# A second ring for the values' pages, moved head stores and loads, and shifted operands in a hybrid attention block

## The chip, the cores and the metric

The kernel runs on one core of one Trainium2 chip. The metric is the device time of one execution in microseconds (us). A kernel's time is the median of its runs; beside it stands one execution taken with the hardware profiler, which has a time of its own.

## What is computed

One layer of a streaming encoder over 512 tokens with 2048 channels, all in float32:

```python
h = rms_norm(x, norm_mix_w)
q_a, k_a, v_a, q_g, k_g, v_g, r_g, gate_lr = split(h @ w_in)
y_a = chunked_band_attention(q_a, k_a, v_a, bias)       # 16 heads of 64, softmax
o_g = gated_linear_attention(q_g, k_g, v_g, log_a)      # 4 heads, state passed over chunks of 64
y_g = rms_norm(o_g) * silu(r_g)
x = x + concat(y_a, y_g) @ w_out
u = causal_depthwise_conv(rms_norm(x) @ w_ffn_up)
x = x + (gelu(u_gate) * u_val) @ w_ffn_down
x = x + sigmoid(rms_norm(x) @ w_ple_gate) * (p @ w_ple_proj)
return rms_norm(x)
```

## The kernel before

**Products.** TensorE (PE) is given each large product as Winograd's seven products of 2x2 blocks (names P1, P2, P6, P5, P7, P3, P4). A *unit* is two blocks of 128 output channels by 512 tokens; its seven products are seven *steps*. Every float32 operand is split in two float32r halves, hi and lo, and a product is made of three passes (hi by hi, hi by lo, lo by hi): 24 matmuls of 256 columns. ScalarE (ACT) writes a weight block's hi half into a `wsplit` page, VectorE (DVE) the lo half, two steps ahead of use (`prep_high`, `prep_low`). Partial results wait in PSUM banks `accA`, `accB`, `accC`; `collect` adds them up in the unit's output page `u`.

**Stages.** First `vproj` makes the linear heads' values and a small gate projection, `plr`. The linear stage then runs units 16, then 20 and 21 as a pair, 17, then 22 and 23 as a pair, 18, 8, 19. Units 16 to 19 are keys and queries of the four linear heads, each followed over ten steps by its head's recurrence (`gla_head`), which stores its result `og` in the scratch `ond`. Units 20 to 23 are the attention's values (`value_product`): here the weights stream through the array and the activations are the part held in it, the other way round than everywhere else. Their results go to two pages `vo`, one for each half of the tokens (h = 0 and 1), and then to the scratch `vad`. Units 8 to 11 are output gates: `after_gates` loads a head's result (`on`) from `ond` and multiplies by it. The front stage runs the attention's eight units 0 to 7 (`attend`) and the gates 9 to 11. Four `PP` steps (`embedding`) follow, then the `wo` stage, the feed-forward stages and the last gate stage. i0 is the first step of unit 11; the `PP` steps are i0+7 to i0+10.

**Pages and rings.** Pages of 4 KB a partition are handed out by rings in turn. In the linear and front stages ring `u` has two pages (u0, u1), for the units' outputs and both `vo` pages; ring `x` has one (r6), for `on` and for `tp`, sums of operands on their way to scratch; ring `c` has one (c0). From the end of the attention on, ring `c` has c1, c2, c0, and hands out two `on` pages, `pT` (the embedding's input), and the `pp_o` pages of the embedding's results. A page is written anew only when its last reader, a store's DMA too, is done.

**Order.** PE, ACT and DVE run in the order in which the steps and an `agenda` of (step, place in the step) write the work down. SyncE (SP) and GpSimd (POOL) only start DMAs; their order is set by the framework's scheduler, and each of their queues is worked through in order, an entry that waits holding those behind it.

**Addresses.** A `wsplit` page has 48 columns more than its contents; `SHIFT` says from which column on it is used, 3 by default, 35 for the values, 48 for the embedding. The built program puts these pages at a multiple of 256 bytes plus 192, and the activations' pages, K and Q of the attention at a multiple of 256 plus 128.

Of the kernel before, what the change touches and what calls it, by code (L numbers as in the profile page):

```python
# [15 lines left out]
T = 512  # L16
# [15 lines left out]
PLAIN = ("P1", "P2", "P6", "P5", "P7", "P3", "P4")  # L32
HALVES = ("P1", "P2", "P6", "P7", "P4", "P5", "P3")
RINGS = {"wr": ("r0", "r1", "r2"), "w": ("w0", "w1", "w2")}
SHIFT = {"v": 35, "pp": 48}
SPLIT = (P, 2096)
FRONT_RINGS = {"u": ("u0", "u1"), "c": ("c0",), "x": ("r6",)}
BACK_RINGS = {"u": ("u2", "u3", "u0", "u1"), "c": ("c1", "c2", "c0"), "x": ("x0", "x1")}
# [5 lines left out]
def encoder_block(ctx: ExitStack, tc: tile.TileContext, A, out):  # L44
# [52 lines left out]
    def page(ring, name, dt=F32, shape=(P, 1024)):  # L97
        tags = rings[ring]
        i = counts.get(ring, 0)
        counts[ring] = i + 1  # L100
        tag = tags[i % len(tags)]
        return page_pool(tag).tile(list(shape), dt, tag=tag, name=name)
# [8 lines left out]
    def psum_mm(name):  # L111
        return pm.tile([P, T], F32, tag="mm", name=name)

    def psum_aux(name):
        return aux[0](name)
# [403 lines left out]
    def value_collect(unit, prod):  # L519
        if unit.half == 0:  # L520
            return
        b = PRODUCTS[prod][2]
        tag, t = unit.banks[b]
        unit.lead.left[b] -= 1
        if unit.lead.left[b] == 0:
            banks.append(tag)
        quarter, sign = QUARTERS[prod]
        s, h = int(quarter[1]) - 1, int(quarter[2]) - 1
        if h not in unit.pages:
            unit.pages[h] = page("u", "vo").rearrange("p (j f) -> p j f", j=2)  # L530
        for j in range(2):
            dst, src = unit.pages[h][:, j, s * 256:s * 256 + 256], t[:, j * 256:j * 256 + 256]
            r = (rtok if sign > 0 else gla["minus"])[:, 2 * h + j:2 * h + j + 1]
            if quarter not in unit.have:
                act.activation(dst, src, AF.Copy, scale=r)
            else:
                vec.scalar_tensor_tensor(dst, src, r, dst, ALU.mult, ALU.add)
        unit.have.add(quarter)
# [199 lines left out]
    def attend(unit):  # L738
# [3 lines left out]
        def tile_(name, cols, dt=F32, tag=None, bufs=1):  # L742
            return att[0].tile([P, cols], dt, tag=tag or name, name=name, bufs=bufs)
# [12 lines left out]
        def high():  # L756
            for n in ("Q", "Kh", "Kl"):
                for s in range(2):
                    M[n, s] = tile_(f"{n}{s}", T, F32R)
            for s in range(2):  # L760
                a = slice(s * 64, s * 64 + 64)
                act.activation(M["Q", s][a], o[a, 0, :], AF.Copy, scale=0.125)
                for r in (a, slice(64 - s * 64, 128 - s * 64)):
                    act.activation(M["Kh", s][r], o[a, 1, :], AF.Copy)
# [73 lines left out]

    tails = [None, None]

    def after_gates(unit):
        g, M = unit.u - 8, {}

        def load():
            M["on"] = page("x" if g < 2 else "c", "on").rearrange("p (s t) -> p s t", s=2)
            nc.sync.dma_start(M["on"], ond[g])

        def times():
            vec.tensor_tensor(unit.o, unit.o, M["on"], ALU.mult)

        def pair():
            ops = store_pair(mixd if g < 2 else None, 4 + g, unit.o[:, 0, :], unit.o[:, 1, :])
            if g >= 2:
                tails[g - 2] = ops

        return [(0, 0, load), (0, 1, lambda: vec.tensor_tensor(unit.o, unit.o, rb2, ALU.mult)),
                (0, 2, lambda: act.activation(unit.o, unit.o, AF.Silu)), (1, 1, times), (1, 3, pair)]

    gla = {}
# [21 lines left out]
    def gla_head(unit):  # L881
# [140 lines left out]
        def result():  # L1022
            for vb in range(2):
                vec.scalar_tensor_tensor(M["o"][:, vb, :], M["o"][:, vb, :], gnw[:, vb:vb + 1], M["rg"], ALU.mult, ALU.mult)
            nc.sync.dma_start(ond[hd], M["o"])

        unit.early = gates_begin
        return [(0, 1, normed), (0, 3, keys), (1, 1, queries), (1, 3, shifted), (1, 6, scores), (2, 4, turn), (3, 1, turned),
                (3, 3, masked), (3, 6, updates), (4, 1, states), (4, 6, lambda: outputs(0)), (5, 1, lambda: evict(0)),
                (5, 4, lambda: outputs(1)), (6, 1, lambda: evict(1)), (6, 3, squares_added), (6, 6, mean), (7, 1, root),  # L1030
                (7, 3, root_exact), (8, 1, result)]

    def after_value(unit):
        if unit.half == 0:
            return []

        def store():
            for t in range(TT):
                nc.sync.dma_start(vad[4 * unit.c:4 * unit.c + 4, :, t].rearrange("b p v -> p b v"),
                                  unit.pages[t // 2][:, t % 2, :].rearrange("p (b v) -> p b v", b=4))  # L1040

        return [(1, 0, store)]

    def front_after(unit):
        u = unit.u
# [65 lines left out]
    for st in (linear, front):  # L1111
        for u in st.units:
            if 16 <= u.u < 20:
                items = gla_head(u)
                u.follow = lambda unit, items=items: items
                u.early()

    i0 = base[front.units[-1]]
    for n, p in enumerate(PLAIN):
# [12 lines left out]
    def embedding_split(raw, t):  # L1132
        ps_[:] = [t.rearrange("p h (k t) -> p k h t", k=2)]
        act.activation(t[:, 0, :], raw, AF.Copy)
        vec.tensor_tensor(t[:, 1, :], raw, t[:, 0, :].bitcast(F32), ALU.subtract)

    raws = {}
    agenda[i0 + 2].append((0, lambda: raws.update(p=embedding_load(page("c", "pT")))))
    agenda[i0 + 6].append((1, lambda: embedding_split(raws["p"], xtile("N1", 1, "ps"))))

    def attention_done():
        actx.close()
# [138 lines left out]
    with tc.tile_pool(name="first", bufs=1, side="right") as fp:  # L1281
        first = [fp.tile([P, 2, 1024], F32R, name=f"first{g}") for g in range(2)]
        for c in range(2):
            def evict(t, ps, c=c):
                v = fp.tile([P, T], F32, tag=f"v{t}", name="vo")
                nc.scalar.activation(v, ps, AF.Copy, scale=rtok[:, t:t + 1])
                nc.sync.dma_start(vgd[2 * c:2 * c + 2, :, t].rearrange("b p v -> p b v"), v.rearrange("p (b v) -> p b v", b=2))

            vproj(A["w_v_g"], c, evict, c == 0, operand_step if c else None)

        gl = page("wr", "wgate_r")
        nc.sync.dma_start(gl[:, :256], A["w_gate"])
        glh = page("w", "glh", F32R, SPLIT)
        nc.scalar.activation(glh[:, KD * 32:KD * 32 + 96], ones[:, 0:96], AF.Copy, scale=0.0)
        gl3 = gl[:, :256].rearrange("p (k r) -> p k r", r=16)
        g3 = glh[:, :KD * 32].rearrange("p (k r) -> p k r", r=32)
        nc.scalar.activation(g3[:, :, 0:16], gl3, AF.Copy)
        nc.vector.tensor_tensor(g3[:, :, 16:32], gl3, g3[:, :, 0:16].bitcast(F32), ALU.subtract)
        plr = psum_mm("plr")
        for half in range(2):  # L1300
            for kt in range(KD):
                x = place(kt, half)
                for p in range(2):
                    nc.tensor.matmul(plr[:, half * 256:half * 256 + 256], glh[:, kt * 32:kt * 32 + P], x[:, p, :],
                                     start=kt == p == 0, stop=kt == KD - 1 and p == 1)
# [208 lines left out]
```

## Time and profile before

| | |
|---|---|
| three runs | 2271.64, 2273.04 (median), 2277.34 us |
| the profiled execution's own time | 2276.34 us |
| its span, first to last instruction | 2274.6 us |
| mean granted TensorE clock | 0.988 |
| PE busy | 2208.4 us (97%), 18588 matmul records |
| DVE busy | 1938.3 us (85%) |
| ACT busy | 1345.1 us (59%) |
| DMA | 518.31 MB, 228 GB/s |

A row of the timeline gives start, length, engine, line, operation, output and inputs, shapes and count, and in brackets the engine's idle time just before and what ended it. Operations of the three engines that are kept in order all carry the line of the helper, L64, so they are told apart by their tiles. A matmul record is longer than the distance to the next one, since matmuls overlap; the rate is read from the distance. In the chain of waits a row is a start, a length and what was worked on; a DMA's row runs from its issue to its landing.

### The profile page before, as it was taken

How to read it: one execution, taken by the hardware profiler on the slowest of the kernel's cores; microseconds unless marked ns; L12 is line 12 of the kernel's file. 1: busy time of each engine (PE TensorE's matmuls, PEld its weight loads, DVE VectorE, ACT ScalarE, POOL GpSimd, SP SyncE). 2: the span in 40 equal slices, each digit the busy share in tenths (PEclk: the TensorE clock that was granted, in tenths of full speed). 3: DMA queues.
4: the chain of work that ended last, by engine and by line, in shares of the span. 5: the costliest groups of instructions: out<-in, count | busy, mean ns of one | idle time of the engine just before them, and what ended most of it. 6: DMA issues, size and time to landing. Idle time of an engine off the chain costs nothing.

```text
span 2274.6 us, 46290 instructions
## 1 busy us (share of the span) xinstructions
PE 2208.4 (97%) x18588; PEld 2157.1 (95%) x18588; DVE 1938.3 (85%) x2655; ACT 1345.1 (59%) x2001; POOL 158.3 (7%) x196
## 2 busy tenths in 40 slices
PE   9999999999989999999999999999999999999995
PEld 7898988999979999999999999999999999999995
DVE  8476777999858898999988888888898797999997
ACT  8455556667755575555555555555564554766655
POOL 0000000000000000000000000000000100000000
PEclk9999999999989999999999999999999999999998
DMA  6466655677887997888888888888866967879994
GB/s 226 135 179 183 199 159 154 180 184 197 279 263 239 298 280 199 222 229 225 211 224 212 223 209 226 209 226 211 261 221 230 316 234 247 308 256 322 285 297 155
DMA packets 190760, 518.31 MB, mean 228 GB/s; under 512 B 20272, under 2 KB 66608, under 8 KB 190544
## 3 DMA queue, kind: packets, MB, share of 16 engines
q1 hardware_dynamic: 160272, 415.72, 53.9%
q0 software_dynamic: 25920, 93.33, 23.1%
q10 hardware_dynamic: 4352, 6.29, 0.8%
q8 instruction: 146, 2.39, 0.4%
q14 instruction: 70, 0.57, 0.1%
HBM read 441.86 MB, written 71.30 MB: 226 GB/s over the span
## 4 chain that ended last, share of the span: by engine, by line
PE 81%; DVE 8%; DMA 5%; ACT 3%; issue 2%; SPq 0%; DVEq 0%; ACTq 0%; POOLq 0%
PE accA L64 41%; PE accC L64 21%; PE accB L64 10%; DVE wsplit L64 2%; PE v L239 1%; PE v L240 1%; PE v L241 1%; DVE u L64 1%; DMA s<-in_w_blk 1%; PE ptr L64 1%; PE py L64 1%; PE psc L64 1%; DMA dn_R<-g_R 1%; ACT wsplit L64 1%; PE pp L64 1%
## 5 line engine op out<-in xcount | busy, mean ns | idle before, releaser
L64 ACT ACTIVATE wsplit<-l 128x1024 fp32r<-128x1024 f32 (+1 forms) x476 | 495.4, 1042 | 301.7 <-PE accC L64 122.4
L64 DVE TENSOR_TENSOR wsplit<-l,wsplit 128x1024 fp32r<-128x1024 f32 (+1 forms) x476 | 571.3, 1201 | 108.5 <-ACT wsplit L64 107.4
L64 DVE TENSOR_TENSOR wsplit<-s,wsplit 128x1024 fp32r<-128x1024 f32 (+1 forms) x253 | 303.7, 1201 | 65.2 <-ACT wsplit L64 64.7
L64 ACT ACTIVATE wsplit<-s 128x1024 fp32r<-128x1024 f32 (+1 forms) x253 | 262.6, 1039 | 60.3 <-PE accB L64 32.8
L64 ACT ACTIVATE u<-accA 128x256 f32<-128x256 f32 x302 | 114.1, 378 | 274.2 <-PE accA L64 266.2
L64 PE MATMUL accA<-up_T,wsplit 128*128 128x256 f32 x2112 | 253.2, 276 | 0.0
L64 PEld LDWEIGHTS accA<-up_T,wsplit 128*128 128x128 f32 x2112 | 245.6, 188 | 0.1
L64 DVE SCALAR_TENSOR_TENSOR cv<-u,cw,cv 128x511 f32<-128x511 f32 (+1 forms) x176 | 131.6, 748 | 3.1
L64 PE MATMUL accB<-up_R,wsplit 128*128 128x256 f32 x1056 | 128.8, 278 | 2.7 <-ACT up_R L64 1.4
L64 PE MATMUL accA<-dn_T,wsplit 128*128 128x256 f32 x1056 | 126.8, 277 | 3.8 <-DVE wsplit L64 2.1
L405 POOL DMA_DIRECT2D s<-in_w_up x88 | 76.1, 865 | 764.6 <-DMA s<-in_w_up 380.7
L64 PEld LDWEIGHTS accB<-up_R,wsplit 128*128 128x128 f32 x1056 | 124.5, 190 | 3.2 <-ACT up_R L64 1.6
L64 PEld LDWEIGHTS accA<-dn_T,wsplit 128*128 128x128 f32 x1056 | 122.8, 188 | 4.8 <-DVE wsplit L64 2.7
L64 PE MATMUL accA<-up_R,wsplit 128*128 128x256 f32 x1056 | 127.0, 276 | 0.0
L64 PE MATMUL accA<-up_N,wsplit 128*128 128x256 f32 x1056 | 126.5, 276 | 0.0
L64 PE MATMUL accC<-up_N,wsplit 128*128 128x256 f32 x1056 | 126.5, 276 | 0.0
L64 PE MATMUL accC<-up_R,wsplit 128*128 128x256 f32 x1056 | 126.5, 276 | 0.0
L64 PEld LDWEIGHTS accA<-up_R,wsplit 128*128 128x128 f32 x1056 | 122.9, 188 | 0.5 <-issue 0.5
L64 PEld LDWEIGHTS accA<-up_N,wsplit 128*128 128x128 f32 x1056 | 122.8, 188 | 0.0
L64 PEld LDWEIGHTS accC<-up_N,wsplit 128*128 128x128 f32 x1056 | 122.8, 188 | 0.0
L64 PEld LDWEIGHTS accC<-up_R,wsplit 128*128 128x128 f32 x1056 | 122.8, 188 | 0.0
L64 PE MATMUL accA<-in_T,wsplit 128*128 128x256 f32 x768 | 98.5, 286 | 11.7 <-ACT u L64 11.7
(337 smaller groups left out, 4257.8 us busy)
## 6 DMA issues: line engine op xcount, KB each, us to landing
l<-in_w_up SPq DMA_DIRECT2D x132, 512.0 KB, 4.5
s<-in_w_up SPq DMA_DIRECT2D x88, 512.0 KB, 5.0
s<-in_w_up POOLq DMA_DIRECT2D x88, 512.0 KB, 6.3
l<-in_w_dn SPq DMA_DIRECT2D x56, 448.0 KB, 5.3
l<-in_w_blk SPq DMA_DIRECT2D x48, 512.0 KB, 4.6
s<-in_w_blk SPq DMA_DIRECT2D x32, 512.0 KB, 4.4
s<-in_w_blk POOLq DMA_DIRECT2D x32, 512.0 KB, 7.6
l<-in_w_out SPq DMA_DIRECT2D x28, 512.0 KB, 5.0
```

Of the source, the lines that this page charges most:

```text
L64: ins = f(*args, **kw)
L239: nc.tensor.matmul(ps[t], x[:, 0, sl], wh, start=kt == 0, stop=False)
L240: nc.tensor.matmul(ps[t], x[:, 0, sl], wl, start=False, stop=False)
L241: nc.tensor.matmul(ps[t], x[:, 1, sl], wh, start=False, stop=kt == KD - 1)
L405: nc.gpsimd.dma_start(t, src("L22" if name == "S1" else "L11"), accum_op=ALU.add)
```

## The change

The values' weights move from column 35 to 29 of their pages. Each of the two Q tiles of the attention gets 64 columns more and is used from column 19 on. The `vo` page of the second token half comes from ring `x`. The loads of `on` move from the step after a gates unit to steps inside it; the stores of `og` and of the values are written down later. The embedding's input is split one step earlier. `plr` takes its PSUM bank from the other pool.

```diff
-SHIFT = {"v": 35, "pp": 48}
+SHIFT = {"v": 29, "pp": 48}
...
-            unit.pages[h] = page("u", "vo").rearrange("p (j f) -> p j f", j=2)
+            unit.pages[h] = page("x" if h else "u", "vo").rearrange("p (j f) -> p j f", j=2)
...
-                    M[n, s] = tile_(f"{n}{s}", T, F32R)
+                    M[n, s] = tile_(f"{n}{s}", T + 64 * (n == "Q"), F32R)
+                    if n == "Q":
+                        M[n, s] = M[n, s][:, 19:19 + T]
...
+    def load_heads(unit):
+        g = unit.u - 8
+        unit.M = {"on": page("x" if g < 2 else "c", "on").rearrange("p (s t) -> p s t", s=2)}
+        nc.sync.dma_start(unit.M["on"], ond[g])
+
     def after_gates(unit):
-        g, M = unit.u - 8, {}
-
-        def load():
-            M["on"] = page("x" if g < 2 else "c", "on").rearrange("p (s t) -> p s t", s=2)
-            nc.sync.dma_start(M["on"], ond[g])
+        g, M = unit.u - 8, unit.M
...
-        return [(0, 0, load), (0, 1, lambda: vec.tensor_tensor(unit.o, unit.o, rb2, ALU.mult)),
+        return [(0, 1, lambda: vec.tensor_tensor(unit.o, unit.o, rb2, ALU.mult)),
...
-            nc.sync.dma_start(ond[hd], M["o"])
...
-                (7, 3, root_exact), (8, 1, result)]
+                (7, 3, root_exact), (8, 1, result), (10, 0, lambda: nc.sync.dma_start(ond[hd], M["o"]))]
...
-        return [(1, 0, store)]
+        return [(2, 0, store)]
...
+            elif 8 <= u.u < 12:
+                agenda[base[u] + (3, 3, 6, 3)[u.u - 8]].append((0, lambda u=u: load_heads(u)))
...
-    agenda[i0 + 6].append((1, lambda: embedding_split(raws["p"], xtile("N1", 1, "ps"))))
+    agenda[i0 + 5].append((1, lambda: embedding_split(raws["p"], xtile("N1", 1, "ps"))))
...
-        plr = psum_mm("plr")
+        plr = psum_aux("plr")
```

In bytes: the part held in the array stands, modulo 256, at 204 in ordinary products (192 plus 3 columns of 4 bytes) and the streaming part at 128, 76 apart. In the values' products the held part stands at 128 and the streaming part at 76 before (192 plus 35 columns), at 52 now: a distance of 52 before and of 76 now. In the attention's scores Q is held and K streams: both at 128 before, Q at 204 now, so 0 before and 76 now.

The order of PE and of POOL is the same in both programs; ACT and DVE differ in the place of the embedding's split alone, and SP in that of two `on` loads. The first piece is of SP at the end of the front stage, before: behind the loads of the `wo` stage's activations (`wo_R`, `wo_T`) stands unit 11's `on`.

```order
L325 DMA wo_R_7161<-mix_R_120 128x1024
L325 DMA wo_R_7163<-mix_R_121 128x512
L325 DMA wo_T_7202<-mix_T_128 128x1024
L325 DMA wo_T_7204<-mix_T_129 128x512
L846 DMA on<-ond 128x1024
L404 DMA s_7255<-in_w_out 128x1024
```

And SP of the changed kernel, fourteen entries earlier in the same queue:

```order
L325 DMA wo_R_7007<-mix_R_118 128x1024
L402 DMA l_6974<-in_w_out 128x1024
L325 DMA wo_R_7009<-mix_R_119 128x512
L846 DMA on<-ond 128x1024
L402 DMA l_7014<-in_w_out 128x1024
L402 DMA l_7019<-in_w_out 128x1024
L325 DMA wo_N_7048<-mix_N_126 128x1024
```

The load of `on` has passed nine loads of activations and five of weights; all of these now stand behind it.

The second place is ACT at the first products of unit 17, right behind the first pair of value units, with the semaphores each entry waits for; before:

```order
L64 ACTIVATE vo<-accA,minus 128x256
L64 ACTIVATE wsplit<-l_1562 128x1024 [waits DVE_49,Activation_49]
L64 ACTIVATE u<-accA 128x256 [waits DMAHW2_49,DMAHW3_49,PE_49,Activation_49]
L64 ACTIVATE wsplit<-s_1641 128x1024 [waits DMASW6_49]
L64 ACTIVATE e<-pz,cols 128x512 [waits PE_49]
```

and of the changed kernel:

```order
L64 ACTIVATE vo<-accA,minus 128x256
L64 ACTIVATE wsplit<-l_1562 128x1024 [waits DVE_49,Activation_49]
L64 ACTIVATE u<-accA 128x256 [waits PE_49]
L64 ACTIVATE wsplit<-s_1641 128x1024 [waits DMASW6_49,Activation_49]
L64 ACTIVATE e<-pz,cols 128x512 [waits PE_49]
```

The first write of unit 17's `u` waited for two DMAs (the stores of `vo`, whose page it takes over) and now waits for PE alone; the same holds for unit 18 behind the second pair.

The third place is SP behind the second pair, in the changed kernel: unit 8's `on`, which stood far ahead before (behind unit 16's store of `og`), is between the two token halves' stores of `vo`.

```order
L402 DMA l_2516<-in_w_blk 128x1024
L1041 DMA vad<-vo 128x4x128 x2
L846 DMA on<-ond 128x1024
L1041 DMA vad<-vo 128x4x128 x2
L404 DMA s_2638<-in_w_blk 128x1024
```

The first two stores are those of the page in r6, which `on` takes next. The stores of `og` stand at the same places in both queues.

## The prediction

> **What bounds the kernel now.** First the page: how long PE is busy, and what the chain that ended last consists of.
>
> ```profile
> span 2274.6 us, 46290 instructions
> PE 2208.4 (97%) x18588; PEld 2157.1 (95%) x18588; DVE 1938.3 (85%) x2655; ACT 1345.1 (59%) x2001; POOL 158.3 (7%) x196
> PE 81%; DVE 8%; DMA 5%; ACT 3%; issue 2%; SPq 0%; DVEq 0%; ACTq 0%; POOLq 0%
> ```
>
> PE is idle for only 66 us, and the chain is on PE for 81% of the span. A window over all that follows the front stage shows where it is full, and windows of the step from the front stage to `wo` where it is not (columns: length, then busy time of PE, PEld, DVE, ACT, POOL, the granted clock, DMA share, GB/s).
>
> ```profile
> 680.00:2240.00 1560.00, 1546.68 (x13552) 1542.03 (x13552) 1388.46 (x1655) 904.05 (x1247) 117.62 (x136) 1.00 0.84 245
> 600.00:620.00 20.00, 19.47 (x171) 19.15 (x169) 19.67 (x25) 16.07 (x21) 0.00 (x0) 1.00 1.01 364
> 632.00:635.00 3.00, 0.00 (x0) 0.00 (x0) 0.00 (x0) 0.00 (x0) 0.00 (x0) 1.00 1.07 278
> 635.00:643.00 8.00, 0.00 (x0) 0.00 (x0) 1.86 (x2) 0.56 (x2) 0.00 (x0) 0.53 0.72 236
> 643.00:649.00 6.00, 5.91 (x14) 4.65 (x15) 2.81 (x5) 5.01 (x11) 1.31 (x2) 0.50 0.74 180
> ```
>
> From 680 to 2240 us PE works for all but 13 us; the change moves nothing there, so what is won before should reach the end whole. Winnings come from two sources: PE's holes before 660 us, and faster matmuls. The holes that the change touches are taken one by one, in profiled time.
>
> **The bank of `plr`.** Timeline rows of PE around the first linear unit:
>
> ```profile
> 103.89 1.98 PE L1304 MATMUL plr<-in_R,glh 128*128 128x256 f32 x16
> 105.91 0.68 DVE L1310 TENSOR_TENSOR lr<-plr,rb 32x512 f32<-32x512 f32 x1 [4.30 <-PE plr L1304]
> 106.64 3.00 PE L64 MATMUL accA<-in_R,wsplit 128*128 128x256 f32 x24 [0.77 <-DVE lr L1310]
> ```
>
> `accA` waits until DVE has read `plr` out of the same bank. With `plr` elsewhere the 0.77 us go; what needs `lr`, `pz`, comes 2.7 us later. **0.8 us.**
>
> **The waits on the values' stores.** Rows of ACT, DVE and PE behind the first pair (unit 17), then of the second (unit 18):
>
> ```profile
> 176.75 2.88 PE L64 MATMUL accA<-in_R,wsplit 128*128 128x256 f32 x24
> 183.78 0.38 ACT L64 ACTIVATE u<-accA 128x256 f32<-128x256 f32 x1 [5.04 <-DMA vad<-vo]
> 186.95 0.41 DVE L64 TENSOR_TENSOR u<-u,accB 128x256 f32<-128x256 f32 x1
> 191.01 1.22 DVE L64 TENSOR_TENSOR wsplit<-s,wsplit 128x1024 fp32r<-128x1024 f32 x1
> 192.24 0.36 ACT L64 ACTIVATE u<-accA 128x256 f32<-128x256 f32 x1
> 192.65 2.99 PE L64 MATMUL accA<-in_T,wsplit 128*128 128x256 f32 x24 [2.73 <-ACT u L64]
> 249.67 2.88 PE L64 MATMUL accA<-in_R,wsplit 128*128 128x256 f32 x24
> 254.56 0.39 ACT L64 ACTIVATE u<-accA 128x256 f32<-128x256 f32 x1 [2.90 <-DMA vad<-vo]
> 263.44 3.00 PE L64 MATMUL accA<-in_T,wsplit 128*128 128x256 f32 x24 [1.48 <-ACT u L64]
> ```
>
> ACT could read P1 at 179.65, when PE is done, and stands until the store of `vo` has landed; everything behind it in ACT's order slips by 4.1 us. Without that wait the next limit is DVE: it adds P2 once PE has made it, at 183.5 instead of 186.95, and from there its chain (difference of the DVE rows, 5.3 us with the end of the last) and ACT's short pieces let P7 start at about 189.25. PE itself, with four products of 2.8 us and `pz`'s 1.05 from 176.75 on, is done at 189.0. So 192.65 becomes 189.25: 3.4 us. Behind the second pair the same sum gives 262.1 for 263.44: 1.3 us. **4.7 us.** The new place of unit 8's `on` adds a wait to SP: it needs r6, so it stands until the first two stores have landed, and two stores and a weight load stand behind it.
>
> ```profile
> 244.70 7.60 SPq L1039 DMA_DIRECT2D vad<-vo  x4
> 257.18 2.47 SPq L404 DMA_DIRECT2D s<-in_w_blk  x2
> DMA to landing us min/median/max: 3.3/6.6/9.7
> ```
>
> Issued at 245, landed by 255 at the latest, and the weight load behind comes at 257.18: nothing. If that cover were gone, each microsecond would delay the weight load by one. The stores of `og` keep their place, so their edit costs and brings nothing.
>
> **The operands' places.** Chain rows of the first pair's last products, of an ordinary product and of scores:
>
> ```profile
> 159.88 5.68 PE accA L64 x48
> 195.64 2.72 PE accC L64 x24
> 468.48 0.95 PE psc L64 x8
> ```
>
> The same matmul of 256 columns takes 118.3 ns in the values' products and 113.3 ns in ordinary ones, at the same clock. The distance of the two operands is what differs: 52 bytes modulo 256 against 76. In the scores it is 0, and 8 matmuls of 256 columns take 118.8 ns each. The trace has no streaming part at 52, so it does not show the new pair itself: between 5.0 ns less and the slowest distance seen, 118.8. I take the full rate, as the distance becomes that of the ordinary row. The lower bound is a loss of 0.5 ns on 672, 0.3 us. There are 4 units of 7 products of 24, 672 matmuls; 5.0 ns on 576 of them are 2.9 us; the 96 of P1 win nothing, because DVE ends last there:
>
> ```profile
> 133.38 0.69 DVE L64 SCALAR_TENSOR_TENSOR eb<-u,eb 128x512 f32<-128x512 f32 x1
> 134.12 0.49 PE L64 MATMUL pat<-eb,en 128*128 128x128 f32 x2
> ```
>
> The scores' 16 matmuls a unit, in eight units, save about 0.1 us a unit (0.95 to 0.907, and less on the wider ones): 0.8 us. **3.7 us**, bounds -0.3 and 4.2. The Trainium skill's page SBUF — State Buffer, section "Who interferes with whom", gives TensorE two independent read ports, one for the moving operand and one for the weights, and says that it never waits on anyone. By that rule the shifts bring nothing and the sum below is 2258.0; the 118.3 beside 113.3 ns at full clock do not agree with it.
>
> **The last head's load.** Rows of the chain, then of DVE, ACT and PE:
>
> ```profile
> 609.12 7.75 DMA wo_N<-mix_N
> 627.22 13.89 DMA on<-ond
> 620.60 0.63 ACT L64 ACTIVATE wo_N<-wo_N 128x512 fp32r<-128x512 f32 x1 [0.81 <-DMA wo_N<-mix_N]
> 641.13 1.23 DVE L64 TENSOR_TENSOR u<-u,on 128x1024 f32<-128x1024 f32 x1 [10.44 <-DMA on<-ond]
> 642.44 1.09 ACT L64 ACTIVATE pp_o<-pp 128x512 f32<-128x512 f32 x2 [12.06 <-DVE u L64]
> 620.84 10.95 PE L64 MATMUL pp<-ps,wsplit 128*128 128x512 f32 x47 [1.37 <-DVE ps L64]
> 643.09 14.03 PE L64 MATMUL pp<-ps,wsplit 128*128 128x512 f32 x48 [11.31 <-ACT pp_o L64]
> 656.96 3.24 PE L64 MATMUL accA<-wo_R,wsplit 128*128 128x256 f32 x27
> ```
>
> Unit 11's `on` is issued at 627.22 behind the `wo` loads and lands at 641.1; DVE stands for it, ACT's `pp_o` for its page, PE for the bank. At its new place it goes out at about 609.1 and lands near 617. Three things go: 11.3 us of standing; 2.7 us that the half clock costs afterwards (the window has 14 matmuls in 5.91 us, 422 ns each, where 47 in 10.95 are 233); and the 1.37 us for `ps`, whose split moves one step ahead. From 619.1 (620.84 less that wait and the one matmul before it) four steps of 5.44 us (the 47 are two, less their overlap) end at 640.9, 16 us before 656.96. What is late next takes part of that back. `on` pushes the `wo_N` loads back by one transfer of 512 KB, about 1.3 us of a full queue: ACT's `wo_N` moves from 620.6 to 621.9, and with 2.3 us of its work in between `pp_o` begins at 624.2: PE loses 0.3. `pp_o` of the second `PP` step still follows `on` in DVE's order, which without its wait is done at 641.13 - 10.44 + 1.23 = 631.9: PE, through with that step at 630.2, stands 2.3 us. Then the pages: each `pp_o` page is reused only when its store has landed, and stores take long while the queue is full.
>
> ```profile
> DMA to landing us min/median/max: 4.1/7.3/13.1
> ```
>
> The second store goes out at 627 and, at the longest of these, lands at 640; PE, through with the third step at 638.0, stands 2.7 us for it in the fourth, and I add 1.3 us for the third store. `wo` starts at 640.9 + 0.3 + 2.3 + 2.7 + 1.3 = 647.5: **9.5 us**, bounds 16 (no standing) and 5 (every store as slow as 13 us and one more half-clock spell).
>
> **Sum.** 0.8 + 4.7 + 3.7 + 9.5 = 18.7 us, from 2276.34 to 2257.6 in profiled time. That execution is 3.3 us above the median of the runs, so the forecast is 2254.3 us.
>
> **Rivals.** *The address does nothing*: the rates stay at 118 ns because it is the streaming part's own start that counts (aligned to 128 bytes in ordinary products, 52 now). Then 3.7 us are missing: 2258 us. *The hole only moves*: PE's short gaps in the `PP` steps draw the half clock again, or the stores hold longer. A rule bears on this:
>
> ```profile
> 310.00:314.00 4.00, 2.40 (x22) 2.20 (x20) 3.97 (x8) 3.95 (x5) 0.00 (x0) 1.00 0.77 228
> 314.00:318.00 4.00, 0.54 (x2) 0.54 (x3) 3.12 (x4) 2.92 (x7) 0.86 (x1) 0.58 0.69 170
> ```
>
> PE worked for 2.40 us of the first window, until 312.4; the clock of the second averages 0.58, so it halved at about 314.6, 2.2 us after. Behind my 2.3 and 2.7 us gaps that would slow some 3.5 us of work by half: 2 to 4 us, and with slower stores 5.5 in all, 2260 us. The Trainium skill's page TensorE: Matmul & The Clock Gate, section "What's actually happening", puts the fall after an idle window of about 3.4 us; by that my gaps draw nothing. The trace agrees at 632 to 635 and not at 314. *The page wait stays*: unit 17 and 18 stand for something else just as late, 2259 us. *Slower*: `on` at its new place holds SP. Behind it stand all later `wo` loads, and ACT already waits for the first of them. If c0, its page, were still being read D us past 609, the loads, ACT's `wo_N` and with them `pp_o` and PE would come D later, one for one: 2254.3 + D. It ends slower by over 0.3% (6.8 us, about what a measurement of this kernel can tell from no change) from D = 26 on; at 30 it gives 2284 us. Against it: the last stores out of c0 go out at 593, and the longest landing quoted here, 13.9 us, makes that 608.
>
> ```profile
> 592.87 1.27 SPq L261 DMA_DIRECT2D mix_R<-yp  x2
> ```
>
> **Chances.** Forecast 0.55; the address 0.15; the hole moves 0.20; the page wait 0.04; slower 0.03; better than forecast, with no stores in the way, 0.03. The range takes the first three with both off together at the top (2254.3 + 3.7 + 5.5 = 2263) and, at the bottom, the 6 us of standing left out and the runs' low end (2246). Faster by over 0.3% (under 2266.2) holds in all but the slower rival and the far ends of two others: 0.92, within 0.05, slower 0.03.
>
> **What would show it.** In the profile after: no `accA` wait on `lr`; no ACT `u` wait on `vad`; the values' 48 matmuls in 5.44 us and 8 scores in 0.91; `on` landing before 620, no PE gap over 3 us among the `PP` steps, and a granted clock of 1.00 there. A `wo` start over 12 us before the old distance from unit 11, or under 6, would prove the last term wrong; rates of 118 ns the third.

## The result, and the profile after

| | before | changed |
|---|---|---|
| median of the runs | 2274.40 us (4 runs, 2271.64 to 2277.34) | 2261.64 us (4 runs, 2261.15 to 2263.57) |
| the same again on another chip | 2274.79 us (9 runs) | 2261.79 us (5 runs) |
| profiled execution, its own time | 2276.34 us | 2261.30 us |

The ratio is 0.9945, with a 95% interval of 0.9928 to 0.9962; on the second chip it was 0.9942 (0.9929 to 0.9955). The changed kernel is faster by 12.8 us, where 2254.3 us and 18.7 us of gain were forecast. The time lies inside the range, close to its upper end.

The page of the changed kernel, and a window over the part that the change does not touch:

```profile
span 2259.6 us, 46287 instructions
PE 2202.8 (97%) x18588; PEld 2151.8 (95%) x18588; DVE 1938.2 (86%) x2655; ACT 1345.1 (60%) x2001; POOL 158.3 (7%) x196
PE 79%; DVE 8%; DMA 7%; ACT 3%; issue 2%; SPq 0%; ACTq 0%; DVEq 0%; POOLq 0%
```

```profile
700.00:2220.00 1520.00, 1507.12 (x13207) 1502.20 (x13207) 1356.49 (x1615) 882.14 (x1217) 115.87 (x134) 1.00 0.84 246
```

PE's busy time fell by 5.6 us only; the rest of the 15.0 us between the two spans is idle time that went. DMA has a larger part in the chain, 7% for 5%. From 700 to 2220 us PE still misses no more than 13 us.

As PE does the same matmuls in the same order, the two traces can be laid side by side. The table takes the starts of the same products in both and the length of each stretch between them:

| stretch, from start to start | before | changed | difference |
|---|---|---|---|
| start to unit 16's first product | 106.64 | 102.75 | -3.89 |
| unit 16 to the first pair | 21.50 | 21.34 | -0.16 |
| first pair of value units | 48.61 | 49.23 | +0.62 |
| unit 17, P1 to P7 | 15.90 | 12.61 | -3.29 |
| unit 17's P7 to unit 18 (with the second pair) | 57.02 | 57.54 | +0.52 |
| unit 18, P1 to P7 | 13.77 | 12.61 | -1.16 |
| to unit 11's last product (front stage) | 352.91 | 352.21 | -0.70 |
| unit 11's last product to `wo` (`PP` steps) | 40.61 | 32.93 | -7.68 |
| `wo` to the feed-forward stage | 153.08 | 154.59 | +1.51 |
| feed-forward to the last matmul | 1448.91 | 1448.13 | -0.78 |

They add up to the 15.0 us. Of the first row 2.95 us had been won by 11.6 us into the span, on matmuls that the change does not touch: in the profiled execution of before the first large products ran 0.43 us a matmul up to 10.9 us, where those of the changed kernel ran 0.23. In a kernel below (e1_places) unit 16 began at 105.47 us, with `plr` changed like here, while in all the other changed ones it began between 102.75 and 103.74. So the comparison by medians, 12.8 us, fits the 12.1 us that remain.

These are the holes that the forecast took first. Timeline rows of the changed kernel, around unit 16, behind the first pair and behind the second (the two rows with 7 matmuls stop where the view's window stops):

```profile
100.93 1.98 PE L1308 MATMUL plr<-in_R,glh 128*128 128x256 f32 x16
102.75 0.96 PE L64 MATMUL accA<-in_R,wsplit 128*128 128x256 f32 x7
...
173.32 3.03 PE L64 MATMUL accA<-in_R,wsplit 128*128 128x256 f32 x24
176.39 0.38 ACT L64 ACTIVATE u<-accA 128x256 f32<-128x256 f32 x1 [1.08 <-PE accA L64]
185.93 3.03 PE L64 MATMUL accA<-in_T,wsplit 128*128 128x256 f32 x24
...
243.47 3.03 PE L64 MATMUL accA<-in_R,wsplit 128*128 128x256 f32 x24
256.08 1.10 PE L64 MATMUL accA<-in_T,wsplit 128*128 128x256 f32 x7
```

`accA` follows `plr` at once. ACT takes up P1 when PE is done with it and waits for no store, and P7 comes 12.61 us after P1 in both units, where it came 15.90 and 13.77 us after it. But look at the lengths: unit 17's P1, an ordinary product, lasts 3.03 us where it lasted 2.88 before, and so does unit 18's.

The values' products in the chain of the changed kernel, to be set against 5.68 us for 48 matmuls before:

```profile
156.20 5.76 PE accA L64 x48
161.96 5.76 PE accC L64 x48
```

They became slower, not faster: 120 ns a matmul for 118.3.

The `PP` steps of the changed kernel, in the timeline, in the chain (a start, a length from issue to landing), and in windows:

```profile
608.29 2.98 PE L64 MATMUL accA<-in_T,wsplit 128*128 128x256 f32 x24
611.11 5.63 PE L64 MATMUL pp<-ps,wsplit 128*128 128x512 f32 x24
618.20 5.74 PE L64 MATMUL pp<-ps,wsplit 128*128 128x512 f32 x24 [1.47 <-ACT pp_o L64]
625.86 7.32 PE L64 MATMUL pp<-ps,wsplit 128*128 128x512 f32 x24 [1.92 <-ACT pp_o L64]
634.81 3.02 PE L64 MATMUL pp<-ps,wsplit 128*128 128x512 f32 x12 [1.63 <-ACT pp_o L64]
638.36 3.02 PE L64 MATMUL pp<-ps,wsplit 128*128 128x512 f32 x12 [0.54 <-ACT pp_o L64]
641.22 5.62 PE L64 MATMUL accA<-wo_R,wsplit 128*128 128x256 f32 x48
648.26 5.72 PE L64 MATMUL accB<-wo_R,wsplit 128*128 128x256 f32 x48 [1.43 <-ACT wsplit L64]
```

```profile
618.66 8.86 DMA ppd<-pp_o
627.60 10.02 DMA ppd<-pp_o
```

```profile
624.00:626.00 2.00, 0.14 (x1) 0.14 (x2) 2.00 (x2) 0.79 (x2) 0.00 (x0) 1.00 1.10 305
626.00:628.00 2.00, 2.00 (x5) 1.58 (x6) 0.26 (x1) 0.29 (x1) 0.00 (x0) 0.50 1.05 271
```

The one hole of 11.3 us became four of 0.5 to 1.9 us, 5.6 us in all, each ended by `pp_o`; two of these stores follow each other in the chain. The third step ran partly at half clock and took 7.32 us for 5.63. And a hole of 1.43 us appeared in `wo`, where there was none: ACT, held back by the late `pp_o`, makes the second `wsplit` too late.

### The profile page after: what moved, and what is told of

It reads as the page before. It is cut to its first block, busy times and chain, and to the rows that moved or that the text cites. A ratio compares the mean times of both kernels' runs of the same rounds, so it can differ in the third digit from the quotient of the medians.

```text
span 2259.6 us, 46287 instructions
## 1 busy us (share of the span) xinstructions
PE 2202.8 (97%) x18588; PEld 2151.8 (95%) x18588; DVE 1938.2 (86%) x2655; ACT 1345.1 (60%) x2001; POOL 158.3 (7%) x196
## 4 chain that ended last, share of the span: by engine, by line
PE 79%; DVE 8%; DMA 7%; ACT 3%; issue 2%; SPq 0%; ACTq 0%; DVEq 0%; POOLq 0%
PE accA L64 40%; PE accC L64 21%; PE accB L64 10%; DVE wsplit L64 2%; PE v L239 1%; PE v L240 1%; PE v L241 1%; DVE u L64 1%; DMA dn_R<-g_R 1%; PE py L64 1%; DMA ppd<-pp_o 1%; PE ptr L64 1%; DMA l<-in_w_ple_gate 1%; PE psc L64 1%; DMA pg_T<-h_T 1%
## 5 line engine op out<-in xcount | busy, mean ns | idle before, releaser
L64 ACT ACTIVATE u<-accA 128x256 f32<-128x256 f32 x302 | 113.8, 377 | 265.6 <-PE accA L64 265.5
```

The costliest lines, as they stand in the source:

```text
L64: ins = f(*args, **kw)
```

## The experiments

Every kernel is the changed one with one edit. Where it says "the step", the time from the start of unit 11's last product to the start of `wo` is meant: 40.61 us before, 32.93 in the changed kernel. It was 32.89 when that was profiled again (e0_after).

A ratio is to the kernel before on the same chip. The runs were made on three chips. On that of e1 to e4 the kernel before took 2278.32 us, on that of e0, e5, e6 and e7 2274.79, and on that of e8 to e11 again 2278.32; the changed kernel itself was timed only on the second of them and on that of the result, where before took 2274.40. So one time in microseconds gives ratios that differ by 0.0017 from chip to chip, and ratios from different chips tell no smaller difference. Four kernels were timed once only: e1_places 2261.40 us, e7_split_late 2264.48, e9_half_stores 2259.28, e11_alternate 2261.79.

### Which place makes a matmul fast (e1_places)

```diff
-            at = SHIFT.get(unit.kind, 3)
+            at = {20: 35, 21: 32, 22: 16, 23: 3}[unit.u] if unit.kind == "v" else SHIFT.get(unit.kind, 3)
...
-                        M[n, s] = M[n, s][:, 19:19 + T]
+                        c = (0, 16, 19, 32, 48, 3, 35, 51)[b]
+                        M[n, s] = M[n, s][:, c:c + T]
```

> The changed kernel with four places for the values' weights (columns 35, 32, 16, 3 for units 20, 21, 22, 23: the streaming part at 76, 64, 0 and 204 modulo 256 bytes, the held part at 128) and eight for Q (columns 0, 16, 19, 32, 48, 3, 35, 51 for units 0 to 7: the held part at 128, 192, 204, 0, 64, 140, 12, 76, the streaming part at 128). Read from the distance of two matmuls of 256 columns. Theory 1, the streaming part must start on a multiple of 64 bytes: 113.3 ns in units 21 and 22, 118 ns or more in 20 and 23; in the scores 118.8 ns in unit 0 alone, 113 to 114 in all others. Theory 2, the distance of the two operands decides, and 76 is the good one: 118 to 120 ns in all four value units; in the scores 113 to 114 in unit 2 alone. Theory 3, a collision once entered is kept until PE stands still, whatever the place: 118 to 121 ns in all four value units and in the first ordinary product behind them, and scores that differ from step to step but not from unit to unit.

Measured, as the mean distance from the ninth matmul of a product to its last: 119.6 ns in unit 20 (column 35), 113.3 in unit 21 (32), 118.9 in unit 22 (16), 117.7 in unit 23 (3). In the scores of 256 columns unit 2, with Q at 204, ran at 113.3 ns; the seven others at 117 to 121. The first ordinary product behind the first pair ran at 119.9 ns throughout, that behind the second at 113.8:

```profile
175.01 3.03 PE L64 MATMUL accA<-in_R,wsplit 128*128 128x256 f32 x24
244.59 2.89 PE L64 MATMUL accA<-in_R,wsplit 128*128 128x256 f32 x24
```

No theory holds whole. Column 16 refutes theory 1: its streaming part is at 0, and it is slow. Column 29 in the changed kernel and column 32 here refute theory 2 for the values: 76 is slow and 64 is fast, though in the scores 76 alone is fast. Theory 3 would explain the ordinary product behind the first pair, which has its usual places and yet runs at 119.9 ns for all its 24 matmuls, until other work interrupts PE. But "whatever the place" is wrong for column 32, and the ordinary product behind the second pair is fast.

### The load of `on` (e2_on_late)

```diff
-        g, M = unit.u - 8, unit.M
+        g, M = unit.u - 8, {}
+        def load():
+            M["on"] = page("x" if g < 2 else "c", "on").rearrange("p (s t) -> p s t", s=2)
+            nc.sync.dma_start(M["on"], ond[g])
...
+        return [(0, 0, load), (0, 1, lambda: vec.tensor_tensor(unit.o, unit.o, rb2, ALU.mult)),
...
-            elif 8 <= u.u < 12:
-                agenda[base[u] + (3, 3, 6, 3)[u.u - 8]].append((0, lambda u=u: load_heads(u)))
```

> The changed kernel with the loads of on back at their old place behind the gates unit. Theory 1, the place of unit 11's load is what shortens the step from the front stage to wo: on lands some 14 us after its issue at about 618, PE stands about 10 us in the PP steps, the clock halves for some 14 us, and wo starts 38 to 40 us after the start of the last product of unit 11 instead of 32.9; the time rises by 5 to 7 us, to about 2268. Theory 2, the earlier split of the embedding's input and the loads' order behind it did it: under 2 us of change, 2262 to 2264.

Measured: median 2268.21 us, ratio 0.9956 (0.9941 to 0.9971); the profiled time is 2266.94 us. Timeline, then chain:

```profile
609.59 11.07 PE L64 MATMUL pp<-ps,wsplit 128*128 128x512 f32 x48
631.02 1.23 DVE L64 TENSOR_TENSOR u<-u,on 128x1024 f32<-128x1024 f32 x1 [11.47 <-DMA on<-ond]
632.98 13.51 PE L64 MATMUL pp<-ps,wsplit 128*128 128x512 f32 x48 [12.33 <-ACT pp_o L64]
646.33 3.92 PE L64 MATMUL accA<-wo_R,wsplit 128*128 128x256 f32 x33
```

```profile
617.10 13.90 DMA on<-ond
```

`on` takes 13.9 us again, DVE stands 11.5 us for it and PE 12.3, and the 48 matmuls behind last 13.51 us for 11.07. The step is 39.55 us, 6.6 us longer. With the `wo` stage behind it, it is 193.5 us, for 187.5 in the changed kernel and 193.7 before, so 6.0 of the 6.2 us that both stretches had won are gone; from unit 16 to unit 18's P7 the stretches are those of the changed kernel within 0.1 us. Theory 1 holds: the place of this load is the largest part of the gain. The intervals of the two ratios overlap, and on one chip the median is 6.9 us above that of e4_pp_pages, whose step is 0.9 us shorter than the changed kernel's.

### The page of the values (e3_vo_ring)

```diff
-            unit.pages[h] = page("x" if h else "u", "vo").rearrange("p (j f) -> p j f", j=2)
+            unit.pages[h] = page("u", "vo").rearrange("p (j f) -> p j f", j=2)
```

> The changed kernel with both vo pages out of the units' ring, as before. Theory 1, the page is what held unit 17 and unit 18: ACT's first u of both waits for the stores again (about 5 and 3 us), P7 of unit 17 starts 3.4 us later, P7 of unit 18 1.3 us later, the time rises by 4 to 5 us, to about 2266. Theory 2, the later place of the stores or the other shift brought it: under 1.5 us of change.

Measured: median 2269.66 us, ratio 0.9959 (0.9944 to 0.9974); the profiled execution, the fastest of the four, took 2265.58 us. Rows behind the first pair (the second stops where the view's window stops):

```profile
180.32 0.38 ACT L64 ACTIVATE u<-accA 128x256 f32<-128x256 f32 x1 [4.56 <-DMA vad<-vo]
189.20 3.17 PE L64 MATMUL accA<-in_T,wsplit 128*128 128x256 f32 x19 [2.73 <-ACT u L64]
```

The wait is back, 4.56 us, and unit 17 takes 15.42 us from P1 to P7 again for 12.61, unit 18 13.76. That is 4.0 us, theory 1; `on` of unit 8 stands at another place in SP's queue here too. Another 1.6 us are lost in between, where neither theory had any: behind the pause of 2.73 us the granted clock fell to 0.50, and unit 17's P7 alone took 4.23 us for 3.03.

### What holds the `PP` steps (e4_pp_pages, e6_pool_stores, e9_half_stores)

The first gives one store more time to land before its page is used again; the second has POOL start the stores besides; the third, on the changed kernel, stores half of the bytes and leaves the other half of this result out.

```diff
-                o = page("c", "pp_o").rearrange("p (s t) -> p s t", s=2)
+                o = page("u" if i and unit.u < 1 else "c", "pp_o").rearrange("p (s t) -> p s t", s=2)
```

> The changed kernel with the second pp_o page of the first PP step taken from the free ring u (u2), so that from there on each page has one store more to land. Theory 1, PE's gaps in the PP steps are the waits of pp_o for its page: the third, fourth and fifth pp_o pages are written 2 to 5 us earlier, the gaps of 1.9 and 1.6 us shrink to under 0.5 us, the spell of half clock goes, and wo starts 3 to 4 us earlier; the time falls to about 2258. Theory 2, the full DMA queue is the limit (wo's activations and weights land when they land): PE stands for wsplit or wo_R instead, and the time changes by under 1 us.

Measured: the step is 31.99 us, 0.9 less; median 2261.33 us, ratio 0.9926 (0.9909 to 0.9942).

```profile
616.85 5.76 PE L64 MATMUL pp<-ps,wsplit 128*128 128x512 f32 x24 [0.43 <-ACT pp_o L64]
622.76 3.01 PE L64 MATMUL pp<-ps,wsplit 128*128 128x512 f32 x12 [0.15 <-ACT pp_o L64]
627.49 3.02 PE L64 MATMUL pp<-ps,wsplit 128*128 128x512 f32 x12 [1.71 <-ACT pp_o L64]
632.34 3.01 PE L64 MATMUL pp<-ps,wsplit 128*128 128x512 f32 x12 [1.84 <-ACT pp_o L64]
637.10 3.04 PE L64 MATMUL pp<-ps,wsplit 128*128 128x512 f32 x12 [1.74 <-ACT pp_o L64]
```

The early gaps shrink as theory 1 has it, and no step runs at half clock, but the gaps behind grow to 5.3 us: the first four stores still land 9 to 14 us after their issue. The 3 to 4 us did not come. The size is that of theory 2, though PE stands for `pp_o` and not for `wsplit` or `wo_R`.

```diff
-                nc.scalar.dma_start(ppd[m % 8:m % 8 + 2, m // 8].rearrange("m p t -> p m t"), o)
+                nc.gpsimd.dma_start(ppd[m % 8:m % 8 + 2, m // 8].rearrange("m p t -> p m t"), o)
```

> The changed kernel with the extra pp_o page of the run before it (e4_pp_pages) and the stores of pp_o started by POOL instead of ACT. Theory 1, ACT stands while it issues these stores (up to 3 us each, for the landing of earlier transfers) and hands that to pp_o and PE: without them PE's gaps in the PP steps fall from 6 us to under 3 and wo starts 3 to 4 us earlier; 2258 us. Theory 2, the full DMA queue lands stores and loads when it can, so the pages are late all the same: wo starts within 1 us of e4_pp_pages.

Measured: the step is 34.35 us, longer by 1.4 than in the changed kernel and by 2.4 than in e4_pp_pages; median 2263.26 us, ratio 0.9944 (0.9932 to 0.9957). ACT no longer stands for an issue, and the first four stores still land 10.2, 11.6, 13.9 and 13.3 us after theirs. Theory 1 is refuted: started by POOL, the stores land no sooner. Theory 2 fits but for its size. One gap grew to 4.11 us, and behind it the last 12 matmuls ran at a granted clock of 0.50 and took 5.48 us for 3.0. In the `wo` stage 1.6 us come back (152.97 us for 154.59), so the two stretches together are as long as in the changed kernel (187.3 for 187.5).

```diff
-                nc.scalar.dma_start(ppd[m % 8:m % 8 + 2, m // 8].rearrange("m p t -> p m t"), o)
+                nc.scalar.dma_start(ppd[m % 8:m % 8 + 2, m // 8, :, 0:256].rearrange("m p t -> p m t"), o[:, :, 0:256])
...
-        nc.sync.dma_start(unit.pp, ppd[unit.u].rearrange("s p t -> p s t"))
+        [nc.sync.dma_start(unit.pp[:, :, c], ppd[unit.u, :, :, 0:256].rearrange("s p t -> p s t")) for c in (slice(0, 256), slice(256, T))]
```

> The changed kernel that stores the embedding's result for the first 256 tokens only (and reads them for both halves later): half the bytes in each store of pp_o, everything else as it is. Theory 1, the gaps in the PP steps are the landings of these stores in a full queue: the stores land 2 to 4 us sooner, the gaps of 6.2 us in all shrink to 3 or less, and wo starts some 30 us after the start of unit 11's last product instead of 32.9. Theory 2, pp_o waits for its turn behind ACT's other work and the loads: under 1 us of change.

Measured: the step is 30.54 us, 2.4 less than in the changed kernel. The first four stores land 8.3, 12.4, 8.8 and 7.8 us after their issue, for 8.9, 13.8, 10.0 and 9.6 in the changed kernel.

```profile
617.25 5.73 PE L64 MATMUL pp<-ps,wsplit 128*128 128x512 f32 x24 [0.93 <-ACT pp_o L64]
624.89 7.37 PE L64 MATMUL pp<-ps,wsplit 128*128 128x512 f32 x24 [1.91 <-ACT pp_o L64]
632.42 3.04 PE L64 MATMUL pp<-ps,wsplit 128*128 128x512 f32 x12 [0.16 <-ACT pp_o L64]
635.63 3.02 PE L64 MATMUL pp<-ps,wsplit 128*128 128x512 f32 x12 [0.17 <-ACT pp_o L64]
638.48 5.62 PE L64 MATMUL accA<-wo_R,wsplit 128*128 128x256 f32 x48
```

The two gaps of the last step are gone, the one behind `on` (1.91) and the half clock are not, and the gaps are 3.2 us in all. Theory 1 holds for the gaps that waited for stores, though these landed only 0.6 to 1.8 us sooner and not 2 to 4. Together the three say: here the queue is full (DMA share 1.05 to 1.10 in the windows above), and of what was tried only fewer bytes made the stores land sooner.

### The split of the embedding's input (e7_split_late)

```diff
-    agenda[i0 + 5].append((1, lambda: embedding_split(raws["p"], xtile("N1", 1, "ps"))))
+    agenda[i0 + 6].append((1, lambda: embedding_split(raws["p"], xtile("N1", 1, "ps"))))
```

> The changed kernel with the embedding's input split one step later, as before. Theory 1, the move is worth the 1.4 us that PE stood for ps: that wait returns behind the first PP matmul and wo starts 1 to 1.5 us later. Theory 2, pp_o's page waits come later and swallow it: the wait for ps returns, the following gaps shrink by as much, and wo starts within 0.4 us.

Measured: the step is 32.59 us, 0.3 less than with the move. Timeline, then windows around the longest gap:

```profile
614.52 10.95 PE L64 MATMUL pp<-ps,wsplit 128*128 128x512 f32 x47 [1.38 <-DVE ps L64]
627.19 3.02 PE L64 MATMUL pp<-ps,wsplit 128*128 128x512 f32 x12 [1.73 <-ACT pp_o L64]
630.46 3.02 PE L64 MATMUL pp<-ps,wsplit 128*128 128x512 f32 x12 [0.26 <-ACT pp_o L64]
636.23 3.01 PE L64 MATMUL pp<-ps,wsplit 128*128 128x512 f32 x12 [2.75 <-ACT pp_o L64]
```

```profile
633.00:636.00 3.00, 0.48 (x3) 0.05 (x1) 2.97 (x8) 2.20 (x5) 0.00 (x0) 1.00 1.02 386
636.00:640.00 4.00, 3.38 (x14) 2.50 (x15) 1.87 (x4) 1.69 (x4) 1.61 (x2) 1.00 1.06 386
```

Theory 2: the wait for `ps` is back, and the steps behind it lose as much less. That part of the change is worth nothing in this step, where `pp_o` ends all the other gaps.

### The places in the time (e0_after, e5_v32, e8_places_back, e10_best, e11_alternate)

> The changed kernel itself, timed beside the kernel before on the chip of the next three runs. All theories: the ratio 0.9945 again, within 0.0015, and the same rates: 120 ns in the values' products, 113.3 in ordinary ones.

Measured: ratio 0.9942 (0.9929 to 0.9955), rates 120 and 113.3 ns.

```diff
-SHIFT = {"v": 29, "pp": 48}
+SHIFT = {"v": 32, "pp": 48}
```

> The changed kernel with the values' weights from column 32 on (streaming part at 64, held part at 128) instead of 29. Theory 1, a place at which the collision dissolves (113 to 114 ns behind the first few matmuls, as unit 21 showed) is worth its difference on PE: 576 matmuls by some 6 ns, 3.4 us, and 0.3 us in the first ordinary products behind the pairs; the time is 3 to 4 us under that of the changed kernel on this chip. Theory 2, in the pairs PE's faster products only wait longer for ACT, DVE and the linear heads' recurrence: 113.6 ns, but the pairs end under 1 us earlier.

Measured: ratio 0.9931 (0.9918 to 0.9945). The values' matmuls ran at 116.5 ns on average, not at the 113.3 of unit 21: counted as in e1_places, at 113.3 in 8 of the 28 products and at 117.8 in the 20 others. The pair takes 48.14 us for 49.23, and unit 18 starts 2.75 us earlier than in e0_after. The stretch from unit 18's P7 to unit 11's last product then took 353.5 us, the longest of all, and the lead at `wo` is 0.1 us. That stretch lies between 350.3 and 353.5 us in the profiles of these kernels, whatever the edit, so one profile does not say that the lead is always lost. Neither theory holds whole: the rate is not that of theory 1, and by unit 18 more was won than the 1 us of theory 2. The median is 2260.73 us, for 2261.79 in e0_after on the same chip, and the intervals overlap.

```diff
-            at = SHIFT.get(unit.kind, 3)
+            at = (35, 32)[unit.u % 2] if unit.kind == "v" else SHIFT.get(unit.kind, 3)
```

> The changed kernel with the values' weights from column 35 in units 20 and 22 and from column 32 in units 21 and 23, whose products alternate. Theory 1, the rate hangs on how a run of matmuls is entered: units 21 and 23 run at 113 to 114 ns behind a few slow ones, though the same column gave 117.8 ns when all four units had it; units 20 and 22 at 118 to 120. Theory 2, the place alone sets it, and the difference between the earlier runs came from other work beside it: 117 to 118 ns in units 21 and 23.

Measured: units 21 and 23 at 114.0 and 113.3 ns, units 20 and 22 at 119.6. With column 32 in all four the second units ran at 116.5. The same operands at the same places run at two rates, and what differed is the place of the weights in the products between: theory 1. The work beside them was not varied by itself. The first ordinary products behind the pairs ran at 119.9 ns here, at 113.5 in e5_v32.

```diff
-SHIFT = {"v": 29, "pp": 48}
+SHIFT = {"v": 35, "pp": 48}
...
-                        M[n, s] = M[n, s][:, 19:19 + T]
+                        M[n, s] = M[n, s][:, 0:T]
```

> The changed kernel with both places undone: the values' weights from column 35, Q from column 0. Theory 1, the forecast's term holds in the end, the places are worth 3 to 4 us: 2265 us. Theory 2, by the rates of the two profiles: values 1 to 1.6 ns faster than in the changed kernel (1.0 us in the pairs and 0.3 behind them), scores of 256 columns 5.4 ns slower (0.4 us), and what PE wins before 250 us is lost again by 380 us: within 1 us of the changed kernel, ratio 0.9935 to 0.9950.

Measured: median 2262.78 us, ratio 0.9935 (0.9919 to 0.9952). Values at 118.9 ns and 113.3 behind the pairs, scores of 256 columns at 118.8. Unit 18 starts 1.45 us earlier than in e0_after, `wo` 0.5 us. The traces refute theory 1: what the places changed up to unit 18 was a loss. By the times no difference from the changed kernel can be told, which was not timed on this chip.

The last one is e5_v32 and e4_pp_pages in one kernel:

> The changed kernel with the values' weights from column 32 and the extra pp_o page (e5_v32 and e4_pp_pages together). Theory 1, the two add up: wo starts 1 us earlier for the pages, PE's faster values bring another 0.3 to 1 us; 1.5 to 2 us under the changed kernel, ratio about 0.9935. Theory 2, the full DMA queue sets the start of wo whatever PE does before: no difference from the changed kernel that can be told, 0.9942.

Measured: ratio 0.9929 (0.9913 to 0.9944), median 2261.31 us; `wo` starts at 638.16 us for 640.85 in e0_after, and the profiled time is 2259.28. It is faster than before beyond doubt; that it beats the changed kernel cannot be told, since the intervals overlap (0.9929 to 0.9955 there).

## Why the prediction was right, and where its sizes were off

| term | forecast | measured, profiled time |
|---|---|---|
| the bank of `plr` | 0.8 | 0.9 |
| the waits on the values' stores | 4.7 | 4.5 |
| the values' place | 2.9 | -1.1 |
| Q's place | 0.8 | 0.4 by the rates |
| the last head's load and what follows | 9.5 | 7.7, and 1.5 given back in `wo` |

**The bank and the page wait** were right in mechanism and in size. Behind the stores' landing DVE's chain was next, as forecast: 3.3 us in unit 17 for 3.4, 1.2 in unit 18 for 1.3. e3_vo_ring brings the wait back, and with it 4.0 us. SP's wait for r6 cost nothing that the traces show.

**The operands' places** are the step that failed: "I take the full rate, as the distance becomes that of the ordinary row". The distance modulo 256 does not set the rate. 76 gives 113.3 ns where activations stream from 128, and 120 where weights stream from 52. The gain of 2.9 us became a loss of 1.1 us, 0.8 us beyond the lower bound. That bound was taken from the scores' 118.8 ns, though the values' own P1 already ran at 120 ns in the trace of before (the first 24 matmuls from 128.14 to 131.02 us). Against e8_places_back, which has the old places, the loss is 1.3 to 1.5 us by unit 18's P7, since the slow first products of units 17 and 18 count too. What the runs show in its place: a run of matmuls can stay at 113.3 or at about 120 ns with the same operands at the same places. Which of the two depends on what ran before (113.5 or 119.9 ns in the same ordinary product, 113.3 or 117.8 in the values at column 32) and on the place. At the ordinary place a product that begins slow after a pause is at 113 within ten matmuls, though without a pause, behind the pairs, it can stay at 119.9 for all 24; at columns 3, 16, 29 and 35 none settled at 113. What in the addresses decides this, and what in the work before, stays open. The rival *the address does nothing*, with its alignment of the streaming part, is refuted as well, by column 16. The Trainium skill's page SBUF — State Buffer, section "Who interferes with whom", gives TensorE two independent read ports and says that it never waits on anyone, which gives no reason for two rates of one product. The runs show two, 113.3 and 120 ns at a granted clock of 1.00, but not where the difference arises.

In the scores the rule came true for 256 columns (113.3 ns for 118.8 from unit 2 on), but not for the wider ones (in the mean 176.7 ns for 175.3 with 384 columns, 230.7 for 232.2 with 512). 64 matmuls by 5.4 ns are 0.35 us, not 0.8. In the time neither place can be seen: without both the ratio is 0.9935.

**The last head's load.** `on` was issued at 601.40 us and landed at 609.43, DVE no longer stood for it, and the start of `wo` came 7.7 us nearer. e2_on_late shows that it is this load: 6.6 of the 7.7 us go with it. So the mechanism was right, and the term was too large. The forecast of what comes late next was close: 6.6 us of standing, 5.6 measured, and for the reasons given, `on` in DVE's order ahead of `pp_o`, then two stores' landings. What is missing are the two costs: 1.7 us of half clock in the third step, which the rival *the hole only moves* had, and 1.4 us in `wo`, which no case had. There ACT's weight pieces, pushed back by the late `pp_o`, meet a PE that starts earlier. With these two, the sum of the term is 6.2 for 9.5. The 1.37 us that the split was to save are the one part of the term that brought nothing (e7_split_late).

**The rival that was nearest** is the pair at the top of the range, both the address and the moved hole, at 2263 us (its sum is 2263.5); 2261.64 was measured. It was given as the corner of two rivals and no chance of its own. Of the 3.3 us by which the profiled execution of before stood above its median, 2.95 lay in its first 11.6 us.

That the time lies in the range is in part luck. In the traces the five terms, with what `wo` gave back, come to some 10.4 us. Another 1.6 us were won in three stretches for which the forecast had no term (0.16, 0.70 and 0.78 in the table), and the last two of these stretches differ by 3.2 and 1.9 us between the profiles of the changed kernel and its variants. Without them the time would be some 2263.3 us, an estimate from these rows, at the very end of the range.

## What to carry to other kernels

A load that is started behind a queue's other loads can cost as much as the queue is long, so look at its place in the queue: 14 entries were 6.6 us here. In the `PP` steps, where the DMA queue was full, another page or another engine to start the store moved the gaps about, and only fewer bytes closed some of them (3.2 us of gaps for 5.6). A rate that goes with an address in one place of a trace is no rule until a run has moved that address alone; and a spacing of matmuls is to be read together with what ran before it.

## What the runs showed of the hardware that was not expected

The same product of 24 matmuls, with the same operands at the same places modulo 256 bytes, the first behind a pair, ran at 113.3 to 113.5 ns a matmul in four profiles (before, e5_v32, e8_places_back, e10_best) and at 119.8 to 119.9 in nine (the changed kernel twice and seven of its variants), for all its length. What differed was the place of the weights in the products ahead of it; in e1_places, where the two pairs had different columns, unit 17 ran at 119.9 and unit 18 at 113.8 in one execution.

The clock halved behind an idle time of 1.92 us (the windows from 624 to 628 us of the changed kernel), and stayed at 1.00 behind one of 2.75 us (the windows of e7_split_late) and behind three of 1.7 to 1.8 in a row (e4_pp_pages, 1.00 in all windows from 614 to 640 us). The pause of 2.73 us before unit 17's P7 is the same in two profiles, and the clock fell behind it in one. Windows of e3_vo_ring, where PE works again from 189.20 us on, then of the kernel before, where it does from 192.65:

```profile
190.00:192.00 2.00, 2.00 (x15) 2.00 (x14) 1.83 (x6) 1.31 (x3) 0.00 (x0) 0.68 0.59 234
192.00:194.00 2.00, 2.00 (x11) 2.00 (x11) 1.28 (x2) 0.53 (x1) 0.86 (x1) 0.50 0.78 207
```

```profile
194.00:196.00 2.00, 2.00 (x20) 2.00 (x19) 1.97 (x6) 1.09 (x2) 0.00 (x0) 1.00 0.66 227
196.00:198.00 2.00, 2.00 (x20) 2.00 (x20) 1.87 (x3) 0.74 (x1) 0.86 (x1) 1.00 0.72 246
```

The length of a pause alone does not decide it. The Trainium skill's page TensorE: Matmul & The Clock Gate, section "What's actually happening", puts the fall after an idle window of about 3.4 us in a window that runs free of the kernel. That the same pause meets it or not would fit a free-running window; that 1.92 us are enough does not.
